# State output with the tables as the stationary operand, and its way back to channels through DRAM

## The chip, the cores and the metric

The kernel runs on one core of a Trainium2 chip. The metric is the device time of one execution in microseconds. Three runs of the kernel before gave a median of 1929.54 us (1927.76 to 1931.59).

## The reference

The reference is a trunk of two layers on one sequence of 512 tokens with 1024 channels, in float32. Each layer adds a half-weighted SwiGLU feed-forward (2816 hidden), then a mixer, then a second feed-forward. The mixer projects the normalised input to q, k, v and u (512 channels each for q and u, 128 for k and v). The q, k, v part is a banded attention with 8 heads. The u part is a state-space model, which is where the change lies:

```
ug = u as 32 groups of 16 channels
x  = ug times B (16 -> 64 complex states per group), forward and backward in time
s  = scan along time: s[t] = a * s[t-1] + x[t]          (complex, per state)
y  = Re(C s) of both directions + d * u                 (64 -> 16 channels per group)
z  = gelu(y)
out = z * sigmoid(z @ w_glu + b_glu)                    (512 x 512)
```

The two normalised results go through one output projection (1024 x 1024), which is added to x.

## The kernel before, in words

Activations lie with channels on the 128 partitions and the 512 tokens along the row. A large product of float32 numbers is made from three products of a rounded format (`mm3`, lines 214 to 218: high by high, high by low, low by high), each 128x128 stationary by 128x512 moving. The weights stream through two raw buffers, are split by ScalarE and VectorE or GpSimd into a high and a low part (`w_split`, lines 189 to 204), and all their loads are issued on the SyncE queue (line 185).

The state-space part works on quarters q = 0 to 3 of 8 groups each. Time is cut into 64 chunks of 8 tokens. Inside a chunk the recurrence is a product with prepared tables, and only the chunk states go through a scan, so a tile has rows (token in the chunk j, channel h) or states, and columns (group g, chunk c). Per quarter there are these steps: `u_in` (8 DMAs that bring the projected u, stored to DRAM before, back as rows (j, h)), `s_load` and `s_load2` (tables from DRAM), `s_in` (products with tables E, line 830), `s_scan` (VectorE scans and rotations, lines 845 to 865), and `s_out` (line 867). `s_out` makes, for each of the 8 groups, three products that accumulate: two state parts with the tables F and the input U with the table TT. In the kernel before, the states (128x64) are the stationary operand and the table (128x128) moves. An even group goes to the columns 0 to 63 of the array and an odd one to 64 to 127 (`tile_position=(0, par * 64)`), and the result has the chunks on the partitions. ScalarE copies it out in two halves, and `y_turn` (line 1036) turns two quarters at a time: 8 transposes on TensorE (line 1041), Gelu on ScalarE straight from PSUM into token order (line 1044), a rounded copy (line 1050) and the low part on VectorE (line 1051). `glu` (line 1090) then makes all 48 products of the 512x512 weight in one step, and sigmoids, products and a sum of squares (`glu_fin`) follow. `norm_ws` (`ws`) is the output projection of this part.

Attention is cut into eight units: `as` (scores, lines 965 to 968, and exponentials on ScalarE, line 975), `an` (division), `ao` (transposes on TensorE, line 998, copied out by lines 1001 and 1003) and `pv` (products with v, line 1013). The list `ORDER` (lines 42 to 46) interleaves the steps of both parts as program order. A planner with its own timing model then orders the instructions of each queue at build time, with program order as priority, so a queue may run a later step first; on the chip each queue runs strictly in the order found. SBUF blocks are handed out in program order by `slot()` and given back by `free()`, and a DMA into a block waits for the block's last reader.

Of the kernel before, what the change touches and what calls it, by code (L numbers as in the profile page):

```python
# [8 lines left out]
F32 = mybir.dt.float32  # L9
F32R = mybir.dt.float32r  # L10
I32 = mybir.dt.int32
AF = mybir.ActivationFunctionType
# [27 lines left out]
N_CONST = 640  # L40

ORDER = """
l0 ui0 pu2 pu3 ui2 ui1 si0 k l1 ui3 v vt q0 si1 sc0 sc1 l2 q1 si2 l3 L0 q2 si3 q3 sc2 L1 so0 L2 as0 sc3 L3 an0
so2 as1 so1 so3 yt0 ao0 yt1 an1 as2 an2 ao1 glu as3 ao2 sn pv0 as4 ws0 an3 ao3 ws1 as5 an4 ws2 ao4 ws3 an5 as6
an6 pv1 ws4 ws5 ao5 as7 ws6 an7 ao7 ao6 pv2 ws7 pv3
""".split()

# [28 lines left out]
class Emit:  # L76
# [678 lines left out]
    def mixer(self, l, st, after):  # L755
# [42 lines left out]


        tabs, Y = {}, {}  # L800

        def s_load(q):
            E, tt = [[self.slot(), self.slot()] for _ in range(2)], [self.slot() for _ in range(3)]
# [63 lines left out]
        def s_out(q):  # L867
            s, F, TT = tabs.pop(q)[2:]
            b = self.bank()
            for gp in range(4):  # L870
                for i, last in ((0, False), (1, False), (2, True)):
                    for par in range(2):
                        g = 2 * gp + par
                        o = b[par * 64:par * 64 + 64, gp * P:(gp + 1) * P]
                        if i < 2:
                            a, f = s[i][:, g * NC:(g + 1) * NC], F[i][g // 4][:, g % 4 * P:(g % 4 + 1) * P]
                        else:
                            a, f = U[q][:, g * NC:(g + 1) * NC], TT[g // 4][:, g % 4 * P:(g % 4 + 1) * P]
                        TE.matmul(o, a, f, start=(i == 0), stop=last, tile_position=(0, par * 64))
            self.free(*F[0], *F[1], *TT, *s, U[q])  # L880
            gh = q // 2
            if q % 2 == 0:
                Y[gh] = [self.slot(), self.slot()]

            for jh in range(2):
                o = Y[gh][jh].rearrange("p (j g h) -> p g j h", j=4, g=8)[:, (q % 2) * 4:(q % 2) * 4 + 4]
                S.copy(o, b.rearrange("p (g j h) -> p g j h", g=4, j=8)[:, :, jh * 4:jh * 4 + 4])
            self.bfree(b)

        def u_proj(m):  # L890
            if m == 2:
# [141 lines left out]

        z = [None] * 4

        def y_turn(gh):
            zf = [self.slot(), self.slot()]
            for jh in range(2):
                b = self.bank()
                for j in range(4):  # L1040
                    TE.transpose(b[:, j * P:(j + 1) * P], Y[gh][jh][:, j * P:(j + 1) * P], self.ident)
                bv = b.rearrange("p (j a c) -> p a j c", j=4, a=2)
                for par in range(2):
                    S.activation(zf[par].rearrange("p (c j) -> p j c", j=8)[:, jh * 4:jh * 4 + 4], bv[:, par],
                                 AF.Gelu_apprx_tanh)
                self.bfree(b)
            self.free(*Y[gh])
            for par in range(2):
                zh, zl = self.slot(1, True), self.slot(1, True)
                S.copy(zh.bitcast(F32R), zf[par])  # L1050
                V.tensor_tensor(out=zl.bitcast(F32R), in0=zf[par], in1=zh, op=B)
                z[gh * 2 + par] = (zf[par], zh, zl)

        def wout(kind, acts, d):
            if d % 4 == 0:
# [31 lines left out]
                (V if m == 1 else Gp).tensor_tensor(out=ss["acc"], in0=ss["acc"], in1=q, op=A)  # L1087
                self.free(q)

        def glu():  # L1090
            sg = []
            wh, wl = self.w_next("glu")
            pg = [self.bank() for _ in range(4)]
            for m in range(4):
                for k in range(4):
                    c = (m * 4 + k) * P
                    self.mm3(pg[m], wh[:, c:c + P], wl[:, c:c + P], z[k][1].bitcast(F32R), z[k][2].bitcast(F32R),
                             k == 0, k == 3)
            for a in z:
                self.free(a[1], a[2])  # L1100
            for m in range(4):
                s = self.slot()
                S.activation(s, pg[m], AF.Sigmoid, bias=self.gains[:, gl + GC_BGLU + m:gl + GC_BGLU + m + 1])
                self.bfree(pg[m])
                V.tensor_tensor(out=s, in0=s, in1=z[m][0], op=M)
                self.free(z[m][0])
                sg.append(s)
                if m:
                    glu_fin(m - 1, sg[m - 1])
            glu_fin(3, sg[3])  # L1110
# [12 lines left out]
        def norm_ws(d):  # L1123
            if d == 0:
# [4 lines left out]
        steps = {"pu": u_proj, "ui": u_in, "k": lambda _: k_proj(), "v": lambda _: v_proj(), "vt": lambda _: v_fin(),  # L1129
                 "l": s_load, "L": s_load2, "q": q_proj, "si": s_in, "sc": s_scan, "so": s_out,  # L1130
                 "as": lambda i: a_scores(*units[i]), "an": lambda i: a_norm(*units[i]),
                 "ao": lambda i: a_out(*units[i]), "pv": a_pv, "yt": y_turn, "glu": lambda _: glu(),
                 "sn": lambda _: s_norm_a(), "ws": norm_ws}
        for x in ORDER:
            n = x.rstrip("0123456789")
# [93 lines left out]
def _tiles(w, cols):  # L1229
# [4 lines left out]


ATT_ORDER = np.array([[(kv * 4 + i) * 64 + dh for kv in range(2) for dh in range(64)] for i in range(4)]).reshape(-1)
SSM_ORDER = np.array([(((gh * 8 + g8) * 2 + gp) * 16 + h) for gh in range(2) for gp in range(2)
                      for g8 in range(8) for h in range(16)])


def _lay_weights(inp):
    out = []
    ar = np.arange
    for kind, a, n in weight_chunks():
        l = a[0]
        if kind == "gu":
            nm = ("ffn1", "ffn2")[a[1]]
            c = ar(a[2] * P, a[2] * P + P)
            blk = np.concatenate([_tiles(inp[nm + "_w_gate"][l], c), _tiles(inp[nm + "_w_up"][l], c)], axis=1)
        elif kind == "dn":  # L1250
            nm = ("ffn1", "ffn2")[a[1]]
            f0, nf, dp = a[2:]
            blk = _tiles(inp[nm + "_w_down"][l][f0 * P:(f0 + nf) * P], ar(dp * 256, dp * 256 + 256))
        elif kind == "u":
            blk = _tiles(inp["w_in"][l], 768 + ar(a[1] * P, a[1] * P + 256))
        elif kind == "kv":
            blk = _tiles(inp["w_in"][l], 512 + ar(256))
        elif kind == "q":
            blk = _tiles(inp["w_in"][l], ATT_ORDER[a[1] * P:a[1] * P + 256])
        elif kind == "wa":  # L1260
            blk = _tiles(inp["w_out"][l][ATT_ORDER], ar(a[1] * P, a[1] * P + 512))
        elif kind == "ws":
            blk = _tiles(inp["w_out"][l][512 + SSM_ORDER], ar(a[1] * P, a[1] * P + 512))
        elif kind == "glu":
            blk = _tiles(inp["ssm_w_glu"][l][SSM_ORDER], SSM_ORDER)
        blk = np.ascontiguousarray(blk).reshape(-1)
        assert blk.size == n * P, (kind, blk.size, n)
        out.append(blk)
    return np.concatenate(out)


def _cols(v):
    return v.reshape(-1, P).T
# [11 lines left out]
def lay(inp):  # L1285
    inp = {k: np.asarray(v) for k, v in inp.items()}
    r = {"w": _lay_weights(inp)}
    r["xt"] = inp["x"][0].T.reshape(KD, P, T).transpose(1, 0, 2)
    g = []
    for l in range(L):  # L1290
        g += [_cols(inp["ffn1_norm"][l]), _cols(inp["mix_norm"][l]), _cols(inp["attn_out_norm"][l][ATT_ORDER]),
              _cols(inp["ssm_out_norm"][l][SSM_ORDER]), _cols(inp["ffn2_norm"][l]), _cols(inp["ssm_b_glu"][l][SSM_ORDER])]
    g.append(_cols(inp["final_norm"]))
    r["gains"] = np.concatenate(g, axis=1)
    r["ident"] = np.eye(P, dtype=np.float32)
    r["sink"] = inp["attn_sink"]
    r["table"] = inp["rel_bias_table"]
    rel = np.arange(-255, 256)
    r["onehot"] = (np.arange(32)[:, None] == _bucket(rel)[None, :]).astype(np.float32)
    r["bandmask"] = np.broadcast_to(np.where(np.abs(rel) <= 128, 0.0, NEG).astype(np.float32), (8, 511))  # L1300
    r["delta"] = np.tile(np.concatenate([np.eye(16), np.zeros((16, 16))]), (4, 1)).astype(np.float32)
    dc = np.zeros((4, 2, 16, L, 8), np.float32)
    dc[:, 0] = inp["ssm_d"].reshape(L, 8, 4, 16).transpose(2, 3, 0, 1)
    r["dcol"] = dc.reshape(P, L * 8)

    def gp(v):
        return v.transpose(1, 3, 0, 2).reshape(P, L, G)

    ldt = np.broadcast_to(inp["ssm_log_dt"][:, :, :, None], (L, 2, G, 64))
    r["s5p"] = np.stack([gp(inp["ssm_a_re"]), gp(inp["ssm_a_im"]), gp(ldt)], axis=2).reshape(P, L, 3 * G)  # L1310
    r["s5bc"] = np.stack([inp["ssm_b_re"].transpose(1, 3, 0, 2, 4).reshape(P, L, T),
                          inp["ssm_b_im"].transpose(1, 3, 0, 2, 4).reshape(P, L, T),
                          inp["ssm_c_re"].transpose(1, 4, 0, 2, 3).reshape(P, L, T),
                          inp["ssm_c_im"].transpose(1, 4, 0, 2, 3).reshape(P, L, T)], axis=2).reshape(P, L, 4 * T)
    return {k: np.ascontiguousarray(v) for k, v in r.items()}
# [44 lines left out]
```

## Time and profile before

| | |
|---|---|
| median of 3 runs | 1929.54 us |
| the profiled execution | 1926.47 us |
| its span in the trace | 1924.7 us |
| TensorE busy / its weight loads busy | 97% / 78% of the span |
| VectorE, ScalarE, GpSimd busy | 58%, 33%, 37% |
| mean granted TensorE clock | 0.984 |

The busy share of TensorE is modelled for overlapping instructions, so idle stretches and the distance from one instruction's start to the next one's are read from the timeline. "Granted clock" is the share of the full 2.4 GHz; 0.50 is the lower level, 1.2 GHz. A float32 product shows as two passes, each with a weight load (PEld) and a MATMUL record; a transpose, or a product of the rounded format, is one pass.

### The profile page before, as it was taken

The page shows a single profiled execution, that of the slowest core. Times are in us where ns is not written, and L with a number is a line of the kernel's source. Part 1 is how long each engine was busy: PE and PEld are TensorE (multiplying, and loading weights), DVE is VectorE, ACT ScalarE, POOL GpSimd, SP SyncE. Part 2 cuts the span into 40 slices and gives each one's busy share as a digit, 9 for nine tenths or more (in the row PEclk, how much of TensorE's full clock was granted, in tenths as well). Part 3 has the DMA queues.
Part 4 walks back from the last instruction along what each step waited for, and adds up shares of the span by engine and source line. Part 5 has one row for each costly group of instructions (what it writes and reads, how often), then busy time and mean ns, then how long its engine had stood idle before and what let it go on. Part 6 is the DMA issues. An engine that isn't in the chain of part 4 may idle for free. (4 is left out here: it accounts for less than half of the span.)

```text
span 1924.7 us, 23787 instructions
## 1 busy us (share of the span) xinstructions
PE 1865.4 (97%) x9416; PEld 1510.5 (78%) x9416; DVE 1123.4 (58%) x1713; ACT 626.5 (33%) x954; POOL 714.8 (37%) x596
## 2 busy tenths in 40 slices
PE   8999999997998999999999999999989999999997
PEld 6888888886767888888878888888766678888886
DVE  8646545569888635355674453436697673434435
ACT  5223223322733323223332222224236342222223
POOL 2049899237233015093483351103452230201102
PEclk9999999998899999999999999999989999999998
DMA  5533434576011223233333234424640122222321
GB/s 202 165 121 123 160 125 156 160 244 229 31 67 61 98 104 121 99 131 115 108 134 114 99 133 129 137 98 142 232 171 23 65 79 98 88 107 82 107 97 46
DMA packets 86232, 231.12 MB, mean 120 GB/s; under 512 B 31160, under 2 KB 38504, under 8 KB 70376
## 3 DMA queue, kind: packets, MB, share of 16 engines
q1 hardware_dynamic: 84888, 228.51, 35.0%
q8 instruction: 74, 1.21, 0.3%
q10 hardware_dynamic: 1232, 1.09, 0.2%
q14 instruction: 38, 0.31, 0.0%
HBM read 201.11 MB, written 34.75 MB: 123 GB/s over the span
## 5 line engine op out<-in xcount | busy, mean ns | idle before, releaser
L216 PE MATMUL psum<-blk,whi 128*128 128x512 f32 (+1 forms) x2446 | 954.4, 393 | 9.7 <-ACT blk L277 6.4
L217 PE MATMUL psum<-blk,whi 128*128 128x512 f32 (+1 forms) x2446 | 953.7, 390 | 8.2 <-DVE blk L283 8.2
L218 PE MATMUL psum<-blk,wlo 128*128 128x512 f32 (+1 forms) x2446 | 952.0, 390 | 1.4 <-DVE wlo L202 0.9
L216 PEld LDWEIGHTS psum<-blk,whi 128*128 128x128 f32 x2446 | 462.0, 189 | 108.6 <-ACT blk L277 6.9
L217 PEld LDWEIGHTS psum<-blk,whi 128*128 128x128 f32 x2446 | 461.2, 189 | 106.3 <-DVE blk L283 12.9
L218 PEld LDWEIGHTS psum<-blk,wlo 128*128 128x128 f32 x2446 | 461.2, 189 | 97.9 <-DVE wlo L202 2.0
L199 ACT CAST whi<-raw 128x1024 fp32r<-128x1024 f32 (+1 forms) x310 | 303.4, 1027 | 683.3 <-PE psum L217 476.1
L202 DVE TENSOR_TENSOR wlo<-raw,whi 128x1024 fp32r<-128x1024 f32 (+1 forms) x288 | 419.2, 1490 | 40.6 <-ACT whi L199 30.7
L381 DVE TENSOR_TENSOR blk<-psum,blk 128x512 f32<-128x512 f32 x88 | 60.6, 691 | 343.7 <-PE psum L218 340.2
L407 POOL TENSOR_TENSOR xtile<-xtile,blk 128x512 f32<-128x512 f32 x64 | 88.1, 1378 | 374.3 <-DVE blk L405 370.1
L405 DVE SCALAR_TENSOR_TENSOR blk<-psum,blk 128x512 f32<-128x512 f32 x94 | 64.9, 690 | 214.9 <-PE psum L218 208.9
L380 ACT ACTIVATE blk<-blk 128x512 f32<-128x512 f32 x88 | 55.4, 632 | 301.9 <-DVE blk L378 297.4
L694 POOL TENSOR_TENSOR blk<-blk,blk 128x512 f32<-128x512 f32 x64 | 86.8, 1367 | 92.5 <-PE psum L707 51.7
L378 DVE TENSOR_TENSOR blk<-psum,blk 128x512 f32<-128x512 f32 x88 | 60.2, 688 | 85.7 <-PE psum L218 85.2
L295 POOL TENSOR_TENSOR blk<-blk,blk 128x512 f32<-128x512 f32 x30 | 45.6, 1518 | 155.1 <-ACT blk L288 154.3
L202 POOL TENSOR_TENSOR wlo<-raw,whi 128x1024 fp32r<-128x1024 f32 x22 | 60.4, 2752 | 110.2 <-ACT whi L199 110.0
L695 POOL TENSOR_TENSOR blk<-blk,blk 128x512 f32<-128x512 f32 x64 | 88.1, 1378 | 29.3 <-PE psum L707 14.4
L697 POOL TENSOR_TENSOR blk<-blk,blk 128x512 f32<-128x512 f32 x49 | 77.7, 1590 | 2.4
L385 DVE TENSOR_TENSOR blk<-blk,blk 128x512 fp32r<-128x512 f32 x88 | 76.4, 870 | 0.7 <-ACT blk L384 0.7
L283 DVE SCALAR_TENSOR_TENSOR blk<-xtile,consts,blk 128x512 fp32r<-128x512 f32 x48 | 58.7, 1239 | 10.6 <-ACT blk L277 10.6
L1068 POOL TENSOR_TENSOR xtile<-xtile,blk 128x512 f32<-128x512 f32 x24 | 33.7, 1425 | 72.8 <-DVE blk L1066 68.1
L295 POOL TENSOR_TENSOR blk<-blk 128x512 f32<-128x512 f32 x12 | 19.1, 1595 | 99.4 <-ACT blk L288 99.2
(227 smaller groups left out, 1343.0 us busy)
## 6 DMA issues: line engine op xcount, KB each, us to landing
raw<-w SPq DMA_DIRECT2D x123, 1024.0 KB, 4.8
raw<-w SPq DMA_DIRECT2D x32, 896.0 KB, 4.5
fd<-blk SPq DMA_DIRECT2D x32, 256.0 KB, 2.7
ed<-blk SPq DMA_DIRECT2D x32, 256.0 KB, 3.4
blk<-ed SPq DMA_DIRECT2D x32, 256.0 KB, 5.9
blk<-fd SPq DMA_DIRECT2D x32, 256.0 KB, 4.3
tb<-blk SPq DMA_DIRECT2D x12, 512.0 KB, 2.9
blk<-tb SPq DMA_DIRECT2D x24, 256.0 KB, 6.3
```

What stands on the lines that cost most here:

```text
L199: self.S.copy(hi[:, c], raw[:, c])
L202: eng.tensor_tensor(out=lo[:, c], in0=raw[:, c], in1=hi[:, c].bitcast(F32), op=ALU.subtract)
L216: t.matmul(out, wh, xh, start=start, stop=False)
L217: t.matmul(out, wh, xl, start=False, stop=False)
L218: t.matmul(out, wl, xh, start=False, stop=stop)
L295: eng.tensor_tensor(out=acc, in0=acc, in1=sq, op=ALU.add)
L385: V.tensor_tensor(out=lo.bitcast(F32R), in0=s, in1=hi, op=ALU.subtract)
L405: V.scalar_tensor_tensor(t, ps, 0.5, R, op0=ALU.mult, op1=ALU.mult)
L407: (V if last else self.G).tensor_tensor(out=self.x[d], in0=self.x[d], in1=t, op=ALU.add)
L694: Gp.tensor_tensor(out=full(o), in0=mat(a), in1=pwo(w, 0), op=M)
L695: Gp.tensor_tensor(out=full(t), in0=mat(b), in1=pwo(w, 1), op=M)
L697: Gp.tensor_tensor(out=o, in0=o, in1=t, op=sg)
```

## The change

In `s_out` the operands trade places: the table (128x128) becomes stationary and the states (128x64) move, without a tile position. The result has rows (j, h) and columns (g, c). One ScalarE copy moves it to SBUF, 8 DMAs on the SyncE queue store it to a DRAM tile in an order in which a row is a channel, and a new step `y_in` loads it back (one DMA of 256 KB). `y_turn` is replaced by `y_act` for each quarter: no transposes, one Gelu over 128x512 from SBUF, the rounded copy and the low part. The products of `glu` are made in two steps, `ga` for quarters 0 to 2 (36 products) and `gb` for quarter 3 (12 products), both into the same four PSUM banks. In `ORDER`, `so1` comes before the table loads `L3`, and `as3` and `ao2` come before `gb`. The weights lose a permutation that the old layout needed; their sizes stay.

```diff
-l0 ui0 pu2 pu3 ui2 ui1 si0 k l1 ui3 v vt q0 si1 sc0 sc1 l2 q1 si2 l3 L0 q2 si3 q3 sc2 L1 so0 L2 as0 sc3 L3 an0
-so2 as1 so1 so3 yt0 ao0 yt1 an1 as2 an2 ao1 glu as3 ao2 sn pv0 as4 ws0 an3 ao3 ws1 as5 an4 ws2 ao4 ws3 an5 as6
+l0 ui0 pu2 pu3 ui2 ui1 si0 k l1 ui3 v vt q0 si1 sc0 sc1 l2 q1 si2 l3 L0 q2 si3 q3 sc2 L1 so0 yi0 L2 as0 sc3 so1 yi1 L3 an0
+so2 yi2 as1 yt0 so3 yi3 ao0 yt1 an1 as2 an2 yt2 ao1 ga as3 yt3 ao2 gb sn pv0 as4 ws0 an3 ao3 ws1 as5 an4 ws2 ao4 ws3 an5 as6
...
+        yd = self.dram.tile([4, P, T], F32, name=f"yd{l}")
...
         def s_out(q):
...
-            for gp in range(4):
-                for i, last in ((0, False), (1, False), (2, True)):
-                    for par in range(2):
-                        g = 2 * gp + par
-                        o = b[par * 64:par * 64 + 64, gp * P:(gp + 1) * P]
...
-                        TE.matmul(o, a, f, start=(i == 0), stop=last, tile_position=(0, par * 64))
+            for g in range(8):
+                gc, gk = slice(g * NC, (g + 1) * NC), slice(g % 4 * P, (g % 4 + 1) * P)
+                for i, (x, f) in enumerate(((s[0], F[0]), (s[1], F[1]), (U[q], TT))):
+                    TE.matmul(b[:, gc], f[g // 4][:, gk], x[:, gc], start=(i == 0), stop=(i == 2))
             self.free(*F[0], *F[1], *TT, *s, U[q])
...
-            for jh in range(2):
-                o = Y[gh][jh].rearrange("p (j g h) -> p g j h", j=4, g=8)[:, (q % 2) * 4:(q % 2) * 4 + 4]
-                S.copy(o, b.rearrange("p (g j h) -> p g j h", g=4, j=8)[:, :, jh * 4:jh * 4 + 4])
+            t = self.slot()
+            S.copy(t, b)
             self.bfree(b)
+            dst = yd[q].rearrange("(g h) (j c) -> j h g c", h=16, j=8)
+            for j in range(8):
+                SP.dma_start(out=dst[j], in_=t[j * 16:(j + 1) * 16].rearrange("h (g c) -> h g c", c=NC))
+            self.free(t)
+
+        def y_in(q):
+            Y[q] = self.slot()
+            SP.dma_start(out=Y[q], in_=yd[q])
...
-        def y_turn(gh):
...
+        def y_act(q):
+            zf, zh, zl = self.slot(), self.slot(1, True), self.slot(1, True)
+            S.activation(zf.rearrange("p (c j) -> p j c", j=8), Y[q].rearrange("p (j c) -> p j c", j=8), AF.Gelu_apprx_tanh)
+            self.free(Y[q])
+            S.copy(zh.bitcast(F32R), zf)
+            V.tensor_tensor(out=zl.bitcast(F32R), in0=zf, in1=zh, op=B)
+            z[q] = (zf, zh, zl)
...
-        def glu():
+        pg = []
+
+        def glu(ks):
+
+            if not pg:
+                self.wg = self.w_next("glu")
+                pg.extend(self.bank() for _ in range(4))
+            wh, wl = self.wg
             for m in range(4):
-                for k in range(4):
+                for k in ks:
...
+            if 3 not in ks:
+                return
```

## Rows read from the trace of the kernel before

**Rows 1.** Page, part 1: busy time, share of the span and instructions of each engine.

```profile
PE 1865.4 (97%) x9416; PEld 1510.5 (78%) x9416; DVE 1123.4 (58%) x1713; ACT 626.5 (33%) x954; POOL 714.8 (37%) x596
```

**Rows 2.** Stretches, first layer: length; PE, PEld, DVE, ACT, POOL busy; clock; DMA; GB/s.

```profile
455.00:475.00 20.00, 13.80 (x147) 10.65 (x147) 19.23 (x30) 5.10 (x8) 17.08 (x11) 0.82 0.59 181
475.00:490.00 15.00, 13.29 (x120) 11.23 (x118) 12.55 (x25) 6.12 (x22) 7.49 (x5) 0.67 0.45 164
490.00:500.00 10.00, 9.78 (x72) 7.52 (x69) 7.88 (x24) 9.95 (x21) 0.00 (x0) 1.00 0.01 2
500.00:520.00 20.00, 18.89 (x75) 12.03 (x74) 14.96 (x30) 17.88 (x37) 3.77 (x2) 0.98 0.07 21
```

**Rows 3.** The same view, second layer.

```profile
1420.00:1430.00 10.00, 7.12 (x50) 5.79 (x50) 8.81 (x17) 1.98 (x4) 9.71 (x7) 0.67 0.67 212
```

**Rows 4.** The line of the state output's products: records, duration in ns (min/median/max).

```profile
L879 PEld LDWEIGHTS psum<-blk,blk x368: 132/137/232, 456.0 to 1441.0; 128*64 128x64 f32 x184
L879 PE MATMUL psum<-blk,blk x368: 272/273/476, 456.0 to 1441.1; 128*64 128x128 f32 x184
```

**Rows 5.** Timeline of PE, second layer: start, length, instruction, count, [idle before <-releaser].

```profile
1438.73 2.62 PE L879 MATMUL psum<-blk,blk 128*64 128x128 f32 x44 [1.52 <-DVE blk L856]
1441.28 0.99 PE L998 MATMUL psum<-consts,blk 128*128 128x128 f32 x7
...
1443.87 0.44 PE L965 MATMUL psum<-blk,blk 128*128 128x384 f32 x1 [1.05 <-ACT blk L1044]
```

**Rows 6.** Lines with other numbers of stationary or moving columns, duration in ns.

```profile
L325 PEld LDWEIGHTS psum<-consts,blk x88: 186/192/193, 23.3 to 1911.3; 128*128 128x128 f32 x88
...
L830 PE MATMUL psum<-blk,blk x512: 219/222/370, 418.3 to 1416.5; 128*64 128x64 f32 x171
```

**Rows 7.** Timeline of PE: full-width weight loads with short moving operands, then transposes.

```profile
1477.19 0.95 PE L325 MATMUL psum<-consts,blk 128*128 128x1 f32 x8
...
1478.00 1.07 PE L998 MATMUL psum<-consts,blk 128*128 128x128 f32 x8
...
1478.83 0.48 PE L216 MATMUL psum<-blk,whi 128*128 128x512 f32 x1
```

**Rows 8.** Timeline of the first layer: the last VectorE step before `so3`, and PE.

```profile
486.59 0.69 DVE L856 TENSOR_TENSOR blk<-blk,blk 64x512 f32<-64x512 f32 x1
...
487.95 3.40 PE L879 MATMUL psum<-blk,blk 128*64 128x128 f32 x56
491.28 1.09 PE L998 MATMUL psum<-consts,blk 128*128 128x128 f32 x8
```

**Rows 9.** Timeline of ACT, first layer: table load, Gelu, rounded copy.

```profile
490.58 1.28 ACT L1044 ACT_TABLE_LOAD   x1
...
493.82 1.17 ACT L1044 ACTIVATE blk<-psum 128x256 f32<-128x256 f32 x2
494.74 1.19 ACT L1050 CAST blk<-blk 128x512 fp32r<-128x512 f32 x2
```

**Rows 10.** Timeline of the SyncE queue, first layer: issues, with their length together.

```profile
410.16 3.65 SPq L778 DMA_DIRECT2D blk<-ud  x8
...
462.84 7.47 SPq L815 DMA_DIRECT2D blk<-fd  x4
```

**Rows 11.** Page, part 6: DMA issues, KB each, median us to landing.

```profile
blk<-s5bc SPq DMA_DIRECT2D x8, 256.0 KB, 2.9
ud<-blk SPq DMA_DIRECT2D x8, 256.0 KB, 2.2
...
kd<-blk SPq DMA_DIRECT2D x16, 72.0 KB, 5.6
```

**Rows 12.** Timeline of PE, first layer: the last products of `glu`, the first of `ws`.

```profile
508.98 0.39 PE L217 MATMUL psum<-blk,whi 128*128 128x512 f32 x1
509.20 0.39 PE L218 MATMUL psum<-blk,wlo 128*128 128x512 f32 x1
...
519.24 0.80 PE L216 MATMUL psum<-blk,whi 128*128 128x512 f32 x1 [1.11 <-DVE blk L968]
```

More of the change, by code (lines that the diff above doesn't have):

```diff
@@ L869, in s_out @@
             b = self.bank()
-            for gp in range(4):
-                for i, last in ((0, False), (1, False), (2, True)):
-                    for par in range(2):
-                        g = 2 * gp + par
-                        o = b[par * 64:par * 64 + 64, gp * P:(gp + 1) * P]
[L875 to L878, printed above, removed]
-                        TE.matmul(o, a, f, start=(i == 0), stop=last, tile_position=(0, par * 64))
-            self.free(*F[0], *F[1], *TT, *s, U[q])
-            gh = q // 2
-            if q % 2 == 0:
-                Y[gh] = [self.slot(), self.slot()]
-            for jh in range(2):
-                o = Y[gh][jh].rearrange("p (j g h) -> p g j h", j=4, g=8)[:, (q % 2) * 4:(q % 2) * 4 + 4]
-                S.copy(o, b.rearrange("p (g j h) -> p g j h", g=4, j=8)[:, :, jh * 4:jh * 4 + 4])
-            self.bfree(b)
+            for g in range(8):
+                gc, gk = slice(g * NC, (g + 1) * NC), slice(g % 4 * P, (g % 4 + 1) * P)
+                for i, (x, f) in enumerate(((s[0], F[0]), (s[1], F[1]), (U[q], TT))):
+                    TE.matmul(b[:, gc], f[g // 4][:, gk], x[:, gc], start=(i == 0), stop=(i == 2))
+            self.free(*F[0], *F[1], *TT, *s, U[q])
+            t = self.slot()
+            S.copy(t, b)
+            self.bfree(b)
+            dst = yd[q].rearrange("(g h) (j c) -> j h g c", h=16, j=8)
[5 more added lines that the diff above has]
+            SP.dma_start(out=Y[q], in_=yd[q])
         def u_proj(m):
@@ L1034, in mixer @@
         z = [None] * 4
-        def y_turn(gh):
[L1037 to L1052, printed above, removed]
+        def y_act(q):
[5 more added lines that the diff above has]
+            z[q] = (zf, zh, zl)
         def wout(kind, acts, d):
@@ L1088, in glu_fin @@
                 self.free(q)
-        def glu():
-            sg = []
-            wh, wl = self.w_next("glu")
-            pg = [self.bank() for _ in range(4)]
+        pg = []
[4 more added lines that the diff above has]
+            wh, wl = self.wg
             for m in range(4):
-                for k in range(4):
+                for k in ks:
                     c = (m * 4 + k) * P
@@ L1098, in glu @@
                              k == 0, k == 3)
-            for a in z:
-                self.free(a[1], a[2])
+            for k in ks:
+                self.free(*z[k][1:])
+            if 3 not in ks:
+                return
+            sg = []
             for m in range(4):
@@ L1131, in mixer @@
                  "as": lambda i: a_scores(*units[i]), "an": lambda i: a_norm(*units[i]),
-                 "ao": lambda i: a_out(*units[i]), "pv": a_pv, "yt": y_turn, "glu": lambda _: glu(),
+                 "ao": lambda i: a_out(*units[i]), "pv": a_pv, "yi": y_in, "yt": y_act, "ga": lambda _: glu((0, 1, 2)), "gb": lambda _: glu((3,)),
                  "sn": lambda _: s_norm_a(), "ws": norm_ws}
@@ L1236 @@
 ATT_ORDER = np.array([[(kv * 4 + i) * 64 + dh for kv in range(2) for dh in range(64)] for i in range(4)]).reshape(-1)
-SSM_ORDER = np.array([(((gh * 8 + g8) * 2 + gp) * 16 + h) for gh in range(2) for gp in range(2)
-                      for g8 in range(8) for h in range(16)])
 def _lay_weights(inp):
@@ L1262, in _lay_weights @@
         elif kind == "ws":
-            blk = _tiles(inp["w_out"][l][512 + SSM_ORDER], ar(a[1] * P, a[1] * P + 512))
+            blk = _tiles(inp["w_out"][l][512:], ar(a[1] * P, a[1] * P + 512))
         elif kind == "glu":
-            blk = _tiles(inp["ssm_w_glu"][l][SSM_ORDER], SSM_ORDER)
+            blk = _tiles(inp["ssm_w_glu"][l], ar(512))
         blk = np.ascontiguousarray(blk).reshape(-1)
@@ L1291, in lay @@
         g += [_cols(inp["ffn1_norm"][l]), _cols(inp["mix_norm"][l]), _cols(inp["attn_out_norm"][l][ATT_ORDER]),
-              _cols(inp["ssm_out_norm"][l][SSM_ORDER]), _cols(inp["ffn2_norm"][l]), _cols(inp["ssm_b_glu"][l][SSM_ORDER])]
+              _cols(inp["ssm_out_norm"][l]), _cols(inp["ffn2_norm"][l]), _cols(inp["ssm_b_glu"][l])]
     g.append(_cols(inp["final_norm"]))
```

## The prediction

> **What bounds the kernel now.** The first view is the page's busy time: TensorE is busy 97% of the span, VectorE 58%, ScalarE 33% [rows 1]. So nearly everywhere only fewer or shorter TensorE instructions save time. The change lies in the two mixers, so the second view is the table of stretches there. Between 455 and 490 us of the first layer TensorE is idle 6.2 + 1.7 = 7.9 us and its clock is down (0.82 and 0.67), while VectorE is busy 31.8 of 35 us [rows 2]; the second layer shows the same (7.12 of 10 us busy, 0.67) [rows 3]. That stretch is set by VectorE and by table loads. It ends when VectorE finishes the last scan: in the second layer TensorE stands still 1.52 us until line 856 is done and then runs `so3` [rows 5]; in the first, line 856 ends at 487.3 and the state products run to 491.28 [rows 8]. From there TensorE is bound again: 9.78 of 10 us busy, then 18.89 of 20 [rows 2]. ScalarE is nearly as full there, 9.95 of 10 and 17.88 of 20. So an edit before `so3` can hide in the idle time; an edit from `so3` on counts one for one.
>
> **The products of the state output.** 24 products of two passes are 48 passes a quarter. Before, a pass loads 64 columns and streams 128 [rows 4], and two neighbours work in the two halves of the array: `so3` of the second layer takes 1441.28 - 1438.73 = 2.55 us, 53 ns a pass (44 of 48 records are in the trace) [rows 5]. After, a pass loads 128 columns over the whole array and streams 64. Streaming gets shorter: a record takes 273 ns at 128 columns [rows 4] and 222 at 64 [rows 6], so 51 ns per 64 columns. Loading gets longer: 137 ns at 64 columns [rows 4], 192 at 128 [rows 6], so 55 ns per 64, 110 per 128. Load and stream of successive passes overlap (transposes with both run at (1478.83 - 1478.00) / 8 = 104 ns [rows 7]), so the longer one counts. The trace has no such pass, so the bounds are: below, only streaming counts, 51 ns, 2.4 us a quarter, nothing lost; above, no overlap, 110 + 51 = 161 ns, 7.7 us. The nearest row is line 325, float32 with a 128-column load and one moving column: 8 passes from 1477.19 to 1478.00, 101 ns [rows 7]. I take 105 ns, 5.0 us a quarter, **+2.5 us a quarter** at full clock, 4 quarters and 2 layers.
>
> The rows thus show that the old form is at 53 ns because two products share the array [rows 5]. The Trainium skill, "TensorEngine Tiling (Array Packing)", section "When to Use Tiling", says that for 64 free columns one should swap stationary and streaming and use 2x column tiling, which is what the old form does and the new one undoes. By it the quarter would go from 2.55 to 5.1 us; by a count of streamed columns alone it would fall. The sum above stands on the rows.
>
> Where they fall: `so0` and `so1` (moved before `L3`) lie in the 7.9 us of idle time; I cost them at nothing, and at 5 us a layer if that cover is gone, as when the planner leaves `so1` behind `so2`. `so2` lies in the last 7 us before line 856 ends; partly covered, +1.0 us of its 2.5. `so3` can't start before line 856 and is exposed: **+2.5**.
>
> **Transposes.** `y_turn` goes: 16 a layer at 104 ns [rows 7], 1.7 us. 12 of the 16 stand behind `so3`, so **-1.3**. With them goes TensorE's wait for ScalarE to empty their banks, 1.05 us in the second layer [rows 5]; with nothing taken for the first that is **-0.5** a layer. Of the two-half copies becoming one, and of Gelu on 512 columns (two of 256 take 1.17 us [rows 9]), I expect no change worth counting.
>
> **The way through DRAM.** For quarter 3: copy 0.6 us (as the rounded copy [rows 9]), 8 issues 3.65 [rows 10], landing 2.2, issue and landing of the 256 KB load 0.3 + 2.9 [rows 11], a table load 1.28, Gelu 1.2, rounded copy 0.6 [rows 9], low part 0.7 (as VectorE's row [rows 8]): 13.4 us. The store in 256-byte runs isn't in the trace; its landing lies between 2.2 us and the 5.6 of the scattered `kd` store [rows 11]. I take 2.2, as DMA share there is 0.01 [rows 2] and the `kd` stores run beside other loads. TensorE's cover is what it does between `so3` and `gb`: before, 491.28 to 509.2 with the whole gated product [rows 8, 12], 17.9 us, less 12 products of `gb` at 0.22 to 0.23 (509.20 - 508.98 [rows 12]), 2.7, and the transposes, 1.3, plus what of `as3` and `ao2` is now ahead of `gb`: some 2.5 us, a quarter of the 10 us that stood behind `glu` (509.2 to 519.24 [rows 12]; bounds 0 and 5). That is 16.4 us. So quarter 3 arrives about 3 us early, unless ScalarE, which is full there, adds its own queue. ScalarE gets up to three more table loads (Gelu and Exp now alternate), 3.8 us; I take +0.3 us of TensorE wait. Quarters 0 to 2 have more cover.
>
> The Trainium skill, "DMA: Bandwidth & Descriptors", section "Rules for kernel authors", says that under 64 KB a transfer pays mostly overhead, and its "Specifications" want 512 B for line rate; the eight stores are of 32 KB in 256-byte pieces. By that the landing is nearer to the upper bound and the margin of 3 us is gone; no run here shows it yet.
>
> The 9 new issues a quarter stand in the SyncE queue among the loads of `L2` and `L3` and the weights; a store waits there for ScalarE's copy, and what is behind it waits too. The queue is already held up at 462.84, four issues in 7.47 us [rows 10]. For quarters 0 and 1 this costs table loads up to 4 us each; it is covered as long as the loads for `so3` land before line 856 ends.
>
> **The gated products in two parts.** The same 48 products. But `as3` and `ao2` no longer stand between the last of them and `ws0`. Before, the chain from there (sigmoid, product, `glu_fin`, weights) took those 10 us, with 1.11 us idle [rows 12]. 2.5 us of its cover have moved ahead, so the hole is 1.11 to 3.6 us unless the planner pulls later attention steps in: bounds 0 and +2.5, I take +1.0, since it fills all but 1.1 us now.
>
> **Sum a layer:** 2.5 + 1.0 - 1.3 - 0.5 + 0.3 + 1.0 = +3.0 us, twice +6.0. The profiled execution took 1926.47 us, 1.8 more than its span; it would become 1932.5. The median of the runs is 3.1 above it, 1929.54, so the forecast is **1935.5**, 0.3% slower. A difference below 0.2% (3.9 us) can't be told from none here.
>
> **The rivals.** *All hidden but `so3`* (chance 0.27): the idle time takes `so2` too and the planner fills the hole, 2.5 - 1.3 - 0.5 = +0.7 a layer, 1930.9. For it speaks that 7.9 us of idle are there and that a busier TensorE keeps its clock up; against it that `so2`'s tables come late.
>
> *Faster* (0.15): as y0 to y1 leave early, `ga` products and scores go into the idle time before line 856, so less work is left behind `so3`. It decides when z of quarters 0 and 1 is ready before 487 us, that is `so1` done by about 474 (13.4 us earlier). The price is the 1.52 us of idle [rows 5] or the half clock that stays in the stretch (0.67 over 15 us [rows 2]), some 3 us a layer: 0.7 - 3 = -2.3 a layer, 1924.9. Against it: ScalarE's exponentials and VectorE's chain are ahead of them.
>
> *Much slower* (0.13): TensorE stays at the lower clock through `so2` and `so3`. The stretch 475 to 490 already has 0.67 while the old products run [rows 2]. At 1.2 GHz a pass costs 2 x 105 ns, so each quarter is 10 us; `so3` +7.5 instead of +2.5 is +5 a layer, and with late table loads (SyncE) another +2: 3.0 + 7 = +10 a layer, 1949.5. Against it: the clock was back at 1.00 once TensorE was fed [rows 2].
>
> *That it doesn't do what it says*: if the planner puts `ga`'s products behind quarter 3's arrival, the split is void and the hole after it is as in the forecast; its time lies within the forecast.
>
> **How the numbers follow.** Forecast 0.45, all hidden 0.27, faster 0.15, much slower 0.13. Faster by over 0.2% (below 1925.7): most of the third case, 0.14. Slower by over 0.2% (above 1933.4): the forecast and the last, 0.58; between, 0.28. The forecast's own range is 1931 to 1943 (pass at 101 to 161 ns for `so3`, hole 0 to 2.5). The range 1925 to 1947 leaves out about half of the faster case and half of the much slower.
>
> **What would show it.** Right: the 48 passes take about 5 us a quarter with weight loads back to back, `so3` starts right behind line 856 as before and the next instruction 2.5 us later, no line 1041, and TensorE's idle time between `gb` and `ws0` grows. Wrong: passes at 53 ns or 161; a start of `so3` that moved (then tables or SyncE, not TensorE, are late); a wait of `gb` for quarter 3's low part; idle time before line 856 filled with gated products (faster case); the clock at half in `so3` (much slower).

## The result, and the profile after

The changed kernel took 1980.69 us in the median of 4 runs (1979.31 to 1989.54), the kernel before on the same chip 1928.65 us (1925.71 to 1931.59). The ratio is 1.0278, 95% interval [1.0248, 1.0307]: slower, by 52.0 us between the medians. The profiled execution has a span of 1977.2 us, 52.5 more than before, and a mean granted clock of 0.964.

The page of the changed kernel, busy time of each engine and then the granted clock in 40 slices:

```profile
PE 1917.3 (97%) x9384; PEld 1563.0 (79%) x9384; DVE 1126.8 (57%) x1713; ACT 633.2 (32%) x942; POOL 716.4 (36%) x596
...
PEclk9999999996689999999999999999968999999998
```

TensorE is busy 51.9 us longer than in [rows 1], so all but 0.6 of the 52.5 us is longer work on TensorE, not waiting. The clock row says where: two dips, one in each mixer. An estimate from the mean clocks says how much: 0.036 of 1977.2 us, 71 us, went to the lower clock, against 0.016 of 1924.7, 31 us, before, so some 40 of the 52.5 us are lower clock. The stretches of the first layer (length; PE, PEld, DVE, ACT, POOL busy; clock; DMA; GB/s), cut as in [rows 2]:

```profile
455.00:475.00 20.00, 16.46 (x132) 14.94 (x130) 17.81 (x19) 4.88 (x7) 17.01 (x11) 0.78 0.41 128
475.00:490.00 15.00, 15.00 (x61) 13.21 (x61) 11.84 (x21) 4.21 (x12) 8.72 (x6) 0.50 0.81 243
490.00:500.00 10.00, 10.00 (x38) 8.43 (x38) 4.77 (x21) 2.17 (x9) 0.00 (x0) 0.50 0.33 71
500.00:520.00 20.00, 20.00 (x82) 17.36 (x81) 4.37 (x13) 5.88 (x7) 0.00 (x0) 0.50 0.18 40
520.00:540.00 20.00, 20.00 (x84) 14.14 (x83) 6.83 (x21) 14.75 (x30) 0.00 (x0) 0.90 0.13 27
```

From 475 to 520 us TensorE has no idle time at all and yet stays at 0.50, the 1.2 GHz level. In [rows 2] the same stretch had 0.67, then 1.00. The clock fell behind a wait for a table of `s_in` (a row of PE's timeline, then the stretches around it):

```profile
465.90 2.00 PE L831 MATMUL psum<-blk,blk 128*64 128x64 f32 x32 [2.98 <-DMA blk<-ed]
```

```profile
460.00:465.00 5.00, 2.53 (x42) 2.18 (x41) 4.97 (x3) 1.28 (x2) 3.87 (x3) 1.00 0.66 209
465.00:470.00 5.00, 4.10 (x42) 3.92 (x43) 4.93 (x8) 0.00 (x0) 3.43 (x2) 0.61 0.27 98
```

The kernel before falls there too, and is almost back within 10 us:

```profile
460.00:465.00 5.00, 2.83 (x42) 2.34 (x39) 4.93 (x6) 0.29 (x1) 2.93 (x2) 0.60 0.66 206
...
470.00:475.00 5.00, 3.75 (x27) 2.60 (x28) 4.44 (x16) 1.50 (x3) 4.86 (x4) 0.97 0.67 195
```

What is new is that the clock does not come back. VectorE, which set the pace before, is now idle more than half of the time (busy 4.77 of 10 us, then 4.37 of 20). The timeline of PE shows it pass by pass (start, length, instruction, count), first layer and then second:

```profile
493.48 10.07 PE L875 MATMUL psum<-blk,blk 128*128 128x64 f32 x46
503.35 1.92 PE L998 MATMUL psum<-consts,blk 128*128 128x128 f32 x8
504.92 0.67 PE L965 MATMUL psum<-blk,blk 128*128 128x384 f32 x1
...
510.64 9.91 PE L875 MATMUL psum<-blk,blk 128*128 128x64 f32 x46
520.31 0.77 PE L216 MATMUL psum<-blk,whi 128*128 128x512 f32 x1
...
1475.11 10.07 PE L875 MATMUL psum<-blk,blk 128*128 128x64 f32 x46
1484.98 1.90 PE L998 MATMUL psum<-consts,blk 128*128 128x128 f32 x8
1486.55 0.51 PE L965 MATMUL psum<-blk,blk 128*128 128x384 f32 x1
1487.36 0.44 PE L965 MATMUL psum<-blk,blk 128*128 128x384 f32 x1
...
1489.23 5.25 PE L875 MATMUL psum<-blk,blk 128*128 128x64 f32 x46
1494.28 0.42 PE L965 MATMUL psum<-blk 128*128 128x384 f32 x1
```

A block of 46 of a quarter's 48 new passes (line 875; the other two run ahead of it) takes 9.87 us to the next instruction, 215 ns a pass. So it does in both layers, but for the last quarter of the second: there the clock came back during score products with 384 moving columns (a record of 0.67 us in the first layer, 0.44 here), and the 46 passes took 1494.28 - 1489.23 = 5.05 us, 110 ns a pass, with the clock at 1.00 to their end. By line, the records of the new products and the groups that grew (busy us, mean ns), after and then before:

```profile
L875 PE MATMUL psum<-blk,blk 128*128 128x64 f32 x376 | 75.7, 390 | 0.0
L998 PE MATMUL psum<-consts,blk 128*128 128x128 f32 x160 | 26.6, 304 | 0.0
```

```profile
L879 PE MATMUL psum<-blk,blk 128*64 128x128 f32 x368 | 31.8, 329 | 6.1 <-DMA blk<-fd 4.6 <-DVE blk L856 1.5
L998 PE MATMUL psum<-consts,blk 128*128 128x128 f32 x160 | 22.2, 280 | 0.0
```

With a small second group of 2.5 us on either side (8 records after, 16 before, so that all 384 passes are in both traces) the products take 43.9 us more, the transposes of attention 4.4 and the scores 8.4 (lines 965 and 966 together 60.3 against 51.9). Neither of the last two was changed: they run beside the new products, under the same clock.

Two more places. The way of quarter 3 through DRAM, first layer (copy out, stores, load, Gelu, rounded copy):

```profile
521.57 0.63 ACT L878 COPY blk<-psum 128x512 f32<-128x512 f32 x1
...
522.23 3.64 SPq L883 DMA_DIRECT2D yd<-blk  x8
...
527.46 0.34 SPq L888 DMA_DIRECT2D blk<-yd  x1
...
530.07 1.21 ACT L1038 ACTIVATE blk<-blk 128x512 f32<-128x512 f32 x1 [2.15 <-DMA blk<-yd]
...
531.32 0.62 ACT L1040 CAST blk<-blk 128x512 fp32r<-128x512 f32 x1
```

The low part ends at 532.66, 11.1 us after the copy began, and no product of `gb` waited for it. Behind `gb`, before `ws0`:

```profile
546.12 0.80 PE L216 MATMUL psum<-blk,whi 128*128 128x512 f32 x1 [2.68 <-ACT blk L1069]
549.04 0.79 PE L217 MATMUL psum<-blk,whi 128*128 128x512 f32 x1 [2.13 <-DVE blk L1071]
```

That is 4.8 us of idle time where [rows 12] has 1.11, and the products behind it run at half clock once more (0.63 a record until 554.75).

### The profile page after: what moved, and what is told of

Same layout as the page of the kernel before. It is cut to its first block, busy times and chain, and to the rows that moved or that the text cites. A ratio compares the mean times of both kernels' runs of the same rounds, so it can differ in the third digit from the quotient of the medians.

```text
span 1977.2 us, 23821 instructions
## 1 busy us (share of the span) xinstructions
PE 1917.3 (97%) x9384; PEld 1563.0 (79%) x9384; DVE 1126.8 (57%) x1713; ACT 633.2 (32%) x942; POOL 716.4 (36%) x596
## 5 line engine op out<-in xcount | busy, mean ns | idle before, releaser
L202 DVE TENSOR_TENSOR wlo<-raw,whi 128x1024 fp32r<-128x1024 f32 (+1 forms) x288 | 424.0, 1507 | 40.5 <-ACT whi L199 30.7
L407 POOL TENSOR_TENSOR xtile<-xtile,blk 128x512 f32<-128x512 f32 x64 | 88.1, 1378 | 374.3 <-DVE blk L405 370.1
L875 PE MATMUL psum<-blk,blk 128*128 128x64 f32 x376 | 75.7, 390 | 0.0
L875 PEld LDWEIGHTS psum<-blk,blk 128*128 128x128 f32 x376 | 73.6, 302 | 1.9 <-issue 0.9
```

What stands on the lines that cost most here:

```text
L202: eng.tensor_tensor(out=lo[:, c], in0=raw[:, c], in1=hi[:, c].bitcast(F32), op=ALU.subtract)
L407: (V if last else self.G).tensor_tensor(out=self.x[d], in0=self.x[d], in1=t, op=ALU.add)
L875: TE.matmul(b[:, gc], f[g // 4][:, gk], x[:, gc], start=(i == 0), stop=(i == 2))
```

## The experiments

Ratios are against the kernel before on the same chip, with 95% intervals; its median was 1931.13 us beside the first four, 1929.11 beside the next four, 1929.60 beside the last four. One per cent is 19.3 us.

**e1: the change with the products in their old form.** The chunk layout that follows does not fit the new way, so only its time is read.

```diff
-                    TE.matmul(b[:, gc], f[g // 4][:, gk], x[:, gc], ...)
+                    TE.matmul(o, a, f, start=(i == 0), stop=last, tile_position=(0, par * 64))
```

> The changed kernel (order, way through DRAM, gated products in two parts) with the products of the state output in the old form: states stationary, table moving, two column halves. Rows and columns of the result are then mixed up. Theory 'form' (the new products cost it all: 384 passes took 78 us of TensorE instead of 34, and the granted clock stayed at 0.50 for 55 us while they ran): 1922 to 1936 us, clock as in the kernel before. Rival 'way' (the round trip through DRAM, its issues on the SyncE queue and the new order hold the mixer up, the slow products only fill the wait): 1960 us or more.

Measured: 1942.57 us, 1.0055 [1.004, 1.007], in neither range, but near that of 'form'. **e2** is the reverse, the kernel before with the new products and all else old (again for its time alone):

```diff
-                        TE.matmul(o, a, f, start=(i == 0), stop=last, tile_position=(0, par * 64))
+                    TE.matmul(b[:, gc], f[g // 4][:, gk], x[:, gc], ...)
```

> The kernel before (old order, transposes, gated products in one step) with only the products of the state output in the new form; rows and columns of the result are then mixed up. Theory 'form': 1968 to 1990 us, the clock at 0.50 through most of the state output in both layers. Rival 'way': 1929 to 1945 us (the 2.5 us a quarter of my forecast at full clock, partly hidden).

Measured: 1967.60 us, 1.0192 [1.0177, 1.0207], at the edge of the range of 'form'; 'way' fell. The form alone is worth 1.9% in the old kernel and 2.78% - 0.55% = 2.2% in the new one; the way and the order together 0.55%. e2's stretches, in the order of the columns above, carry the same mark as the change:

```profile
475.00:490.00 15.00, 15.00 (x52) 11.86 (x52) 8.27 (x24) 3.34 (x10) 8.16 (x6) 0.50 0.59 198
490.00:500.00 10.00, 10.00 (x49) 10.00 (x48) 5.21 (x19) 2.71 (x11) 0.00 (x0) 0.50 0.00 0
```

Neither DRAM nor the order is needed for the half clock.

**e3: twice the streaming.** Each table meets the states of two groups, 128 moving columns for 64, so that the sums mix two groups; loads and count stay.

```diff
-                    TE.matmul(b[:, gc], f[g // 4][:, gk], x[:, gc], start=(i == 0), stop=(i == 2))
+                    TE.matmul(b[:, gw], f[g // 4][:, gk], x[:, gw], ...)    # gw: 128 columns, two groups
```

> The changed kernel, but each table is multiplied with the states of two neighbouring groups, 128 moving columns instead of 64 (the sums are then not the reference's): twice the streaming for the same 48 loads of 128 columns a quarter. Theory 'clock' (a pass that streams 64 columns for each 128 loaded leaves the clock at the lower level; at full clock a pass is set by its load, 105 ns, with either width): the granted clock returns in the state output, passes near 107 ns, 1940 to 1962 us, faster than the changed kernel although TensorE streams more. Rival 'start' (the clock is down because TensorE waited before the state output, and the width does not matter): 0.50 as before, passes 210 ns, 1975 to 1990 us.

Measured: 1952.74 us, 1.0107 [1.009, 1.0124]: more arithmetic, and 1.7% faster than the change (33 us by the ratios, 30 by the medians), in the range of theory 'clock'. Its products by form, its timeline of PE in the first layer, and its stretches:

```profile
L875 PE MATMUL psum<-blk,blk 128*128 128x128 f32 x376 | 54.1, 308 | 7.3 <-POOL blk L857 7.2
```

```profile
487.04 8.16 PE L875 MATMUL psum<-blk,blk 128*128 128x128 f32 x46 [2.97 <-POOL blk L857]
498.54 5.30 PE L875 MATMUL psum<-blk,blk 128*128 128x128 f32 x46
```

```profile
490.00:500.00 10.00, 10.00 (x68) 8.88 (x68) 4.14 (x17) 5.54 (x13) 0.00 (x0) 0.88 0.49 114
500.00:520.00 20.00, 20.00 (x109) 15.81 (x107) 10.05 (x31) 15.09 (x25) 0.00 (x0) 1.00 0.18 42
```

The clock rises within the third quarter, which starts at half clock behind a wait of 2.97 us, and the fourth runs at 1.00, 5.30 us, although the loads before each pass are the same. So the half clock is a cost of its own. In the change, in e3 and in the kernel before the clock falls behind a wait; that it then stays low to the end of `so3` is what 64 moving columns in place of 128 bring. The run also shows the bound by loads at full clock: 128 streamed columns cost hardly more than 64 (5.30 against 5.25 us for 46 records). The mean granted clocks of e3 and e1 are nearly the same, 0.981 and 0.979, so e3 against e1, 1.07% - 0.55% = 0.5% or 10 us, is about the price of the loads without the lower clock.

**e4: tables loaded in halves.** Two column tiles of 64 hold the halves of one table, so the result is the change's own.

```diff
-                    TE.matmul(b[:, gc], f[g // 4][:, gk], x[:, gc], start=(i == 0), stop=(i == 2))
+                    for par in range(2):
+                        k0 = g % 4 * P + par * 64
+                        TE.matmul(b[par * 64:par * 64 + 64, gc], f[g // 4][:, k0:k0 + 64], x[:, gc], start=(i == 0), stop=(i == 2),
+                                  tile_position=(0, par * 64))
```

> The changed kernel, with each table loaded as two halves of 64 columns into the two column halves of the array (96 passes a quarter of 64 loaded and 64 streamed columns, in pairs, the shape of the products of s_in, which take 32 ns a pass in the kernel before). The result is the reference's. Theory 'form': 96 x 32 = 3.1 us a quarter at full clock, clock as in the kernel before, 1922 to 1938 us. Rival (any pass with 64 streamed columns holds the clock down): passes near 64 ns, 6.1 us a quarter, clock 0.50 through the state output, 1950 us or more.

Measured: 1944.15 us, 1.0069 [1.0054, 1.0084], between the two ranges; the passes of `so3` and their clock (1.00 from 495 to 500 us) are those of 'form'. The products by form, and the last quarter of the first layer:

```profile
L877 PE MATMUL psum<-blk,blk 128*64 128x64 f32 x752 | 33.4, 256 | 1.8 <-DMA blk<-fd 1.8
```

```profile
495.98 2.90 PE L877 MATMUL psum<-blk,blk 128*64 128x64 f32 x92
```

With twice the passes the block of the last quarter takes 2.90 us instead of 9.91 at half clock or 5.25 at full, 32 ns a pass: two neighbours share the array again. The Trainium skill, "TensorEngine Tiling (Array Packing)", section "When to Use Tiling", asks at 64 moving columns for swapped operands and two column tiles; e1, which has that form, agrees, by 2.2% against the change. e4, with two column tiles and no swap, is no case of that list and gains 2.1%. With the change's layout kept, nearly all of the form's cost is gone, and about 13 us are left.

**What is left: e5 to e8.** I took the idle time between `gb` and `ws0` for it. e5 and e6 are e4 with more put there: `gb` ahead of `as3` and `ao2`, or `an3`, `ao3` and `as5` ahead of `ws0`.

```diff
-... ga as3 yt3 ao2 gb sn pv0 as4 ws0 an3 ao3 ws1 as5 an4 ws2 ...
+e5: ... ga yt3 gb as3 ao2 sn pv0 as4 ws0 an3 ao3 ws1 as5 an4 ws2 ...
+e6: ... ga as3 yt3 ao2 gb sn pv0 as4 an3 ao3 as5 ws0 ws1 an4 ws2 ...
```

> The kernel of e4 (tables loaded in halves) with one change of the order: gb stands before as3 and ao2 again, as the gated product did in the kernel before. Theory 'hole' (of the 11 us that the way and the order cost in e1, most is the wait between gb and ws0, 4.8 us a layer for the scaled high and low parts against 1.1 before, and the clock that falls behind it): the wait shrinks to about 1 us, 1930 to 1938 us. Rival 'arrival' (quarter 3 comes late through DRAM, as3 and ao2 were its cover): gb now waits for quarter 3, 1942 to 1952 us. Rival 'tables' (the loss lies ahead of so3, in loads behind the stores on the SyncE queue): unchanged, 1941 to 1947 us.

> The kernel of e4 with an3, ao3 and as5 moved ahead of ws0, so that more attention work stands between gb and the output projection. Theory 'hole': the wait after gb is filled, 1932 to 1940 us. Rival 'arrival' or 'tables': unchanged, 1941 to 1947 us.

Measured: e5 1956.38 us, 1.0136 [1.012, 1.0153]; e6 1944.34 us, 1.0072 [1.0057, 1.0087]. The theory fell: e5 is 0.7% slower than e4, above all three ranges, and e6 is where e4 was. The rival 'arrival' is hardly seen: no gated product of e5 waits in the first layer, and one waits 0.60 us in the second. The waits change place; behind `gb` the longest in e5 is now that of a score product on ScalarE's copies, and in e6 on VectorE's part of the scores (timeline of PE, one row of each):

```profile
524.65 0.69 PE L968 MATMUL psum<-blk,blk 128*128 128x384 f32 x1 [4.54 <-ACT blk L1006]
```

```profile
525.21 0.69 PE L968 MATMUL psum<-blk,blk 128*128 128x384 f32 x1 [3.19 <-DVE blk L971]
```

e7 is the kernel before with the change's order and nothing else; e8 is e4 with the old order (`so1` behind `as1`, `yt0` behind `so3`, `ga` and `gb` together ahead of `as3`). Besides the two moves that "The change" names, the new order has a third, `yt0` ahead of `so3`: e7 makes it, and e8 takes it back.

```diff
-... L2 as0 sc3 L3 an0 so2 as1 so1 so3 yt0 ao0 yt1 an1 as2 an2 ao1 glu as3 ao2 sn ...
+e7: ... L2 as0 sc3 so1 L3 an0 so2 as1 yt0 so3 ao0 yt1 an1 as2 an2 ao1 as3 ao2 glu sn ...
+e8: ... L2 as0 sc3 L3 an0 so2 yi2 as1 so1 yi1 so3 yi3 yt0 ao0 yt1 an1 as2 an2 yt2 ao1 yt3 ga gb as3 ao2 sn ...
```

> The kernel before with the change's order alone: so1 before L3, as3 and ao2 before the gated product, which stays in one step; old products, transposes, no way through DRAM. The result is the reference's. Theory 'hole': the wait between the gated product and ws0 grows to 4 to 5 us as in e1, 1937 to 1944 us. Rival 'DRAM' (the round trip and its issues on the SyncE queue cost the 11 us): 1927 to 1934 us, no change.

> The kernel of e4 with the whole old order, as far as it can be kept: so1 behind as1, ga and gb together before as3 and ao2. Theory 'hole': as e5, 1930 to 1938 us. If the place of so1 counts (quarter 1 a little later, tables for quarter 3 earlier), it differs from e5 by more than 3 us. Rival 'DRAM': 1942 us or more, since the round trip stays.

Measured: e7 1947.97 us, 1.0093 [1.0078, 1.0108]; e8 1972.63 us, 1.0213 [1.0188, 1.0239]. The new order costs the old way 18 us; the way through DRAM with the old order costs 41. Only together they come to 13. e7 lies above the range of 'hole' and far from 'no change', e8 in that of 'DRAM'.

**Which of the two moves: e9 to e12.** e9 and e10 make one move each in the kernel before, e11 and e12 take one each back in e4.

```diff
+e9:  before, so1 ahead of L3:           ... as0 sc3 so1 L3 an0 so2 as1 so3 yt0 ... ao1 glu as3 ao2 ...
+e10: before, as3 and ao2 ahead of glu:  ... as0 sc3 L3 an0 so2 as1 so1 so3 yt0 ... ao1 as3 ao2 glu ...
+e11: e4, so1 back:                      ... as0 sc3 L3 an0 so2 yi2 as1 so1 yi1 so3 yi3 yt0 ... ga as3 yt3 ao2 gb ...
+e12: e4, gb ahead of as3 and ao2 (e5):  ... as0 sc3 so1 yi1 L3 an0 so2 yi2 as1 yt0 so3 yi3 ... ga yt3 gb as3 ao2 ...
```

> The kernel before with one step of its order moved, so1 ahead of the table loads L3, as the change has it. The whole new order cost the old kernel 19 us (1.0093). Theory A (the table loads are what the order disturbs: so1 waits on VectorE's scan and on the tables, and L3 starts later): this move alone gives most of it, 1.005 to 1.009. Theory B (the scores ahead of glu are what costs, since nothing is left behind glu for the chain to ws0): this move alone costs 0 to 5 us, ratio 0.999 to 1.003.

> The kernel before with the other move of its order alone: as3 and ao2 ahead of glu, so1 in its old place. Theory A: 0 to 5 us, ratio 0.999 to 1.003. Theory B: most of the 19 us of both moves, 1.005 to 1.009, with idle time or a lower clock between glu and ws0.

> The changed kernel with tables loaded by halves (1.0069 with the change's order), so1 and its way back in their old place behind as1, as3 and ao2 still ahead of gb. Theory A: it gains, down to 1.000 to 1.003, since the table loads come as in the kernel before. Theory B: it stays at 1.006 to 1.008 or gets slower, as y of quarter 1 leaves later. With both moves undone the same kernel was at 1.0213.

> The changed kernel with tables loaded by halves, so1 ahead of L3 as in the change, but as3 and ao2 behind gb as they stood behind glu before. Theory A: 1.006 to 1.010, the table loads still disturbed and quarter 3's way through DRAM now uncovered by as3 and ao2. Theory B: it gains, 1.001 to 1.004. If the uncovered way through DRAM is what made 1.0213 with both moves undone, this one is near it, 1.015 to 1.022.

The third move is not with them everywhere: e9 and e10 leave `yt0` behind `so3`, e11 takes it back with `so1`, e12 keeps it ahead.

Measured: e9 1937.39 us, 1.0043 [1.0029, 1.0058]; e10 1927.77 us, 0.9992 [0.9975, 1.0009]; e11 1956.75 us, 1.0148 [1.0124, 1.0172]; e12 1956.48 us, 1.0144 [1.0125, 1.0163]. (e12 is e5's kernel a second time; the two agree.) In the old kernel moving `so1` costs 8 us and moving the scores nothing, which is the way theory A had it, though less than its 1.005. The whole order costs 18 (e7), so some 10 us come from the third move or from the moves together; no run makes the third alone. In the new way the order is needed: without `so1` and `yt0` ahead it is 15 us slower (e11), without the scores ahead 15 (e12), with all of it taken back 28 (e8); theory A fell at e11 and theory B at e12. The third reading of e12, an uncovered way through DRAM (1.015 to 1.022), meets its interval, but in its trace a gated product waits once, for 1.03 us. What `so1` does to the tables shows in e9's SyncE queue (start, length, issues), behind the row of the kernel before, and, in the third fence, on PE:

```profile
474.04 0.38 SPq L815 DMA_DIRECT2D blk<-fd  x1
```

```profile
475.16 0.38 SPq L815 DMA_DIRECT2D blk<-fd  x1
...
489.88 0.32 SPq L815 DMA_DIRECT2D blk<-fd  x1
```

```profile
481.34 1.12 PE L879 MATMUL psum<-blk,blk 128*64 128x128 f32 x8 [4.38 <-DMA blk<-fd]
...
492.90 2.62 PE L879 MATMUL psum<-blk,blk 128*64 128x128 f32 x44 [1.08 <-DMA blk<-fd]
```

The last load of a table F is issued at 489.88, where it was at 474.04 before, and `so3` waits for it: its block runs from 492.90 to 495.45, where the state products before ended at 491.28 [rows 8], 4.2 us earlier.

Lower clock is part of these costs too. By the working of the result's section e4 (mean clock 0.978) lost some 43 us to it against 31 before, 12 of the 20 us between the two profiled spans (1945.0 and 1924.7), and e8 (0.970) some 59. In e4 it lies behind waits: from 480 to 485 us TensorE is busy 1.58 of 5 us, and the clock is 0.51 there and 0.50 in the next 5 us. One wait of e4 is of the way itself, for the rounded copy of quarter 2, first layer:

```profile
510.08 1.49 PE L216 MATMUL psum<-blk,whi 128*128 128x512 f32 x4 [2.17 <-ACT blk L1043]
```

No version here beats the kernel before; e10 can't be told from it.

## Why the prediction was wrong

The direction was right and the mechanism was among the rivals, with a chance of 0.13. By its steps:

**The size of a pass was near, its clock was not.** 105 ns was forecast for full clock, and the one block that ran at it measured 110. The old form was misread by as much: the 44 records of [rows 5] are not 44 of 48 with some lost, four passes ran earlier, so 2.55 us are 58 ns a pass. The two misreadings cancel, and +2.5 us a quarter stands (48 x 52 ns). e3 against e1 puts the loads at 10 us in all, where `so2` and `so3` stood in the sum with 3.5 a layer, 7. The step that failed is the dismissal of *much slower*: "against it: the clock was back at 1.00 once TensorE was fed". In [rows 2] it was, but fed with old passes. With the new ones TensorE had no idle time from 475 to 520 us and stayed at 0.50; e3 changes only the streamed columns and gets 1.00. Of the 2.78%, 1.7% (33 us; 30 by the medians, and 34 by the mean granted clocks of the change and e3) is this clock, 0.5% (10 us) the loads at full clock, 0.55% (11 us) the way and the order. The Trainium skill, "TensorE: Matmul & The Clock Gate", Part 1, has the clock depend on how busy the engine has been; by that the stretch without idle time would run at 2.4 GHz, and here the measurement decides against it.

**The rival's price was right, its extent was not.** It put a quarter at 10 us, as measured (48 x 215 ns), but only for `so3`, +10 a layer: 1949.5 us. The half clock held in the first layer from within `so0` to the end of `so3`, in the second from within `so0` to the end of `so2`, and slowed the scores and transposes between them.

**Cover.** `so0` and `so1` were costed at nothing, under 7.9 us of idle time [rows 2]. At half clock they fill it and more: `so3` ends at 520.31, where the state products ended at 491.28 [rows 8]. The prediction would have read such a moved `so3` as late tables or a late SyncE queue; but no new product waited for anything (idle 0.0 in the group of line 875), the slow passes ahead of it were late. The cover did its part, though: the product, score and transpose records grew by 56.7 us (43.9 + 8.4 + 4.4), the `y` transposes left, and against e1 the change is only 2.2% (some 43 us) slower. e1 is busy as long as the kernel before, within 2.6 us (1868.0), and idle 12.9 us longer; in the change that idle time is filled by slow passes.

**Way and order.** All terms but the products summed to -0.5 a layer (-1.3 - 0.5 + 0.3 + 1.0), -1 us; e1 shows +11. The single pieces were near: the DRAM way of quarter 3 took 11.1 us against 13.4, and `gb` was not held, as forecast (e4's `ga` was, once, by 2.17 us). Three were not. The idle time behind `gb` is 4.8 us in the first layer, beyond the bound of 3.6; yet e5 and e6, which put other work there, gain nothing. Moving `so1` was costed at nothing and is worth 8 us by itself in the old kernel (e9): the condition named, loads for `so3` landed before line 856 ends, did not hold there. In the new way it is not what costs: in e1 the state products wait 4.3 us for tables F, against 4.6 before. And the way needs the new order: without it the cost is 41 us (e8). Where the other 10 us of e7 come from, and which wait carries the last 13 us of e4, stays open: each order leaves waits of a few us on other lines, with lower clock behind them, and no run removed them all.

**The other rivals.** *Faster* asked for gated products before line 856 ends; the idle time there went to slow passes instead. *All hidden but `so3`* counted on a busier TensorE keeping its clock up, which is the same step that failed. Its cover went with it.

## What to carry to other kernels

Before swapping operands, look at what a pass loads and what it streams, and ask for its price at both clocks: here, once a wait had lowered the clock, passes with 128-column loads and 64 moving columns ran at 1.2 GHz with no idle time for 45 us, and their neighbours paid too. Two neighbours in the column halves of the array avoid that with the same layout (e4). An order that fits one way through the kernel is a cost in another, so test the order by itself, and each move alone.

## What the hardware showed unexpectedly

- The passes of the state output, each with a 128-column load and 64 float32 moving columns, with other short products between, ran at a granted clock of 0.50 from 475 to 520 us with TensorE busy throughout. With 128 moving columns the clock rose under way (0.88 from 490 to 500 us, then 1.00). The same 64-column passes, begun at full clock, kept it for the 5 us of the second layer's last block.
- More streaming was faster: 128 columns instead of 64 took some 30 us off the kernel.
- Eight stores of 32 KB in runs of 256 bytes: 3.64 us for the issues, and the load behind them was issued 1.6 us after the last one and arrived 2.6 us later.
